# Channel-major x: first units on un-normed tokens, scaled per token afterwards

## The chip, the cores and the metric

The kernel runs on one core of a Trainium2 chip. The metric is the device time of one execution in microseconds (us), lower is better; three runs of the kernel before gave 838.16 to 839.91 us, median 838.94 us.

The core's engines are named as in the profile: PE (TensorE, matrix products into PSUM), ACT (ScalarE), DVE (VectorE), POOL (GpSimd), SP (SyncE, which here only issues transfers), and 16 DMA engines. Each engine works through its own list of instructions in the order of the program and waits where an operand is not there yet.

## What is computed

One decoder layer on 512 tokens of 1024 channels. All of it starts from one normed input `h`, and every projection is a slice of `h @ w_in`:

```python
def rmsnorm(x, g):
    y = x * lax.rsqrt(jnp.mean(x * x, axis=-1, keepdims=True) + EPS)
    return y * g
...
    h = rmsnorm(x, g_pre[i])
    (gq, gk, gv, ga, gz, dq, dk, dv, iq, ik, iw, dz, xq, xz, gates) = split_cols(h @ w_in[i])
    y_gla = gla_mixer(gq, gk, gv, ga, gz, ...)
    y_dsa = dsa_mixer(dq, dk, dv, iq, ik, iw, dz, rel_bias)
    y_mem = cross_mixer(xq, xz, rmsnorm(mem, g_mem[i]), w_mem_kv[i])
    ...
    x = x + rmsnorm(merged @ w_o[i], g_post[i])
```

The root mean square is a factor per token (a row of x) and `g_pre` a factor per channel (a column), so `(x * g_pre) @ w` multiplied per token by the factor `rstd` is `h @ w`.

## The kernel before, in words

**Arithmetic.** Every large product is taken in three: an operand is split into a high part (ACT copies it to the rounded type, helper `high`, line 95) and a low part (DVE subtracts the high part from the original, helper `low`, line 99 or, with a factor, 101), and high·high, high·low and low·high are added up in one PSUM bank (`mm3`, lines 108 to 110). `split` is `high` followed by `low`. So the list of each engine has the two halves of a split one after the other, and the `low` of DVE waits for the `high` of ACT.

**Units.** The projections are a list of units. A unit takes a weight block of 128 output channels (`unit_t`) or tokens by 256 channels (`unit_n`) and runs in four quarters; a chunk of weights is loaded (`load_next`), split (`split_next`, tiles `whi` and `wlo`) and used. In the loop at the end of `trunk` a unit's quarter is written, then the low halves of weights asked for before (`flush`), then the next weight split (`need`), then after the fourth quarter the unit's evaluation (`done`), then whatever `at(name, quarter, ...)` has put into this slot. Nothing reorders this afterwards: it is the order on every engine.

**The first units** are `dv` (values of the sparse branch), `pc` (a packed unit: indexer keys `ik`, the low-rank gate input `alow`, indexer weights `iw`), `gv0` (values of head 0 of the linear attention, `gv0.0` and `gv0.1`), then the indexer queries `iq0.0`, `iq0.1`, `iq1.0`, `iq1.1` and then `gqk0.0`. Between the quarters of `gv0.1` stand the four `gate_log(h)`: a product `pla` into one of three PSUM banks of the tag "at" (it needs `ar` and `uph`, which `gate_operands` makes), two ACT instructions (`ebig`) and one of DVE (`la_m`), which frees the bank. Unit outputs alternate between two PSUM banks of the tag "mm".

**The prologue** loads x token-major in eight pieces (tiles `x`, 128 tokens by 512 channels), and for each block of 128 tokens squares it on ACT (line 279), takes the power on POOL (273), scales on DVE (287), turns it over to channel-major by eight transposes on PE (294, `xps`) and splits it into `hh` and `hl`. `dv` starts when the first two blocks are turned.

**Transfers** before the loop all stand in SP's list; every one takes one of eight semaphores in turn and waits there for the transfer eight places earlier.

Of the kernel before, what the change touches and what calls it, by code (L numbers as in the profile page):

```python
# [57 lines left out]
def trunk(ctx, tc, x, mem, w_in, w_c, w_kv, w_out, w_o, cols, g_pre, g_mem, g_post, w_up, rel, onehot, out):  # L58
# [134 lines left out]
    def unit_n(name, first, lhs, tiles, done):  # L193

        o = []

        def quarter(q):
            if q == 0:
                o.append(psum("mm", name))
            n = len(tiles)  # L200
            if name[:2] == "dv":
                j, half = divmod(q, 2)
                co = o[0][:, 256 * j:256 * j + 256]
                wh, wl = chunks[first + half][3]
                for p in range(3):
                    for k in range(4):
                        ah, al = lhs(4 * half + k, tiles[j])
                        pe.matmul(co, al if p == 1 else ah, (wl if p == 2 else wh)[:, :, k],  # L208
                                  start=half + p + k == 0, stop=(half, p, k) == (1, 2, 3))
                return  # L210
# [89 lines left out]
    dvh, dvl = kv4("dvh", [4, 256], F32R), kv4("dvl", [4, 256], F32R)  # L300

    def dv_done(i, p):
        p3 = p.rearrange("p (t d) -> p t d", t=2)
        split(dvh[:, 2 * i:2 * i + 2], dvl[:, 2 * i:2 * i + 2], p3)

    win_n("dv", dv_done)
# [723 lines left out]
    xts = [[k2("yh", f"x{tt}{i}") for i in range(2)] for tt in range(4)]  # L1030
    xns = [[k2("acc", f"xn{tt}{i}") for i in range(2)] for tt in range(4)]

    def load_x(tt):
        for i in range(2):
            sp.dma_start(xts[tt][i], x[128 * tt:128 * tt + 128, 512 * i:512 * i + 512])

    with tc.manual_schedule():
        grow = w4("grow")
        sp.dma_start(grow[0:1], g_pre)
        load_x(0)  # L1040
        load_x(1)
        load_next(2)
        load_x(2)
        load_x(3)
# [11 lines left out]
        act.activation(warm[0:1], ones1[:, 0:1], AF.Square)
        gps = [psum("at", "gps") for _ in range(2)]
        for i in range(2):
            pe.matmul(gps[i], ones1, grow[0:1, 512 * i:512 * i + 512], start=True, stop=True)

        def h_scale(tt, ss):
            norm_scale(xts[tt], xns[tt], ss, gps)

        def h_turn(tt, tags=("tp", "tp")):
            t = slice(128 * tt, 128 * tt + 128)
            return norm_turn(xns[tt], lambda i: (hh[:, 4 * i:4 * i + 4, t],
                                                 hl[:, 4 * i:4 * i + 4, t]), tags)
# [18 lines left out]
        low2()
        low3 = h_turn(3, ("at", "ac"))
        low3()
        d0()
# [98 lines left out]
```

## Time and profile before

| | us |
|---|---|
| median of the runs (lowest, highest) | 838.94 (838.16, 839.91) |
| the profiled execution, its own time | 840.41 |
| its span, first to last instruction | 838.7 |
| PE busy in the span | 825.1 |
| first product of `dv` on PE | 12.9 |
| first product of `pc` | 28.2 |
| first product of `iq0.0` | 48.06 |
| first product of `iq1.0` | 56.41 |

The profiled execution ran 1.7 us longer than its span and 1.5 us longer than the median. Times in the rows below are from the start of the span. PE is busy nearly throughout; a wait of PE therefore lengthens the span, and work of the other engines matters where PE waits for it.

### The profile page before, as it was taken

How to read it: one execution, taken by the hardware profiler on the slowest of the kernel's cores; microseconds unless marked ns; L12 is line 12 of the kernel's file. 1: busy time of each engine (PE TensorE's matmuls, PEld its weight loads, DVE VectorE, ACT ScalarE, POOL GpSimd, SP SyncE). 2: the span in 40 equal slices, each digit the busy share in tenths (PEclk: the TensorE clock that was granted, in tenths of full speed). 3: DMA queues.
4: the chain of work that ended last, by engine and by line, in shares of the span. 5: the costliest groups of instructions: out<-in, count | busy, mean ns of one | idle time of the engine just before them, and what ended most of it. 6: DMA issues, size and time to landing. Idle time of an engine off the chain costs nothing.

```text
span 838.7 us, 10810 instructions
## 1 busy us (share of the span) xinstructions
PE 825.1 (98%) x4340; PEld 707.8 (84%) x4340; DVE 471.6 (56%) x839; ACT 329.1 (39%) x597; POOL 51.8 (6%) x77
## 2 busy tenths in 40 slices
PE   7999999999999999999999999999999999999997
PEld 5898888989888888888887888889989898888885
DVE  5578667777676545546677543445645554343623
ACT  5585555353433223334444422434334343322320
POOL 2000101000000020031122000000000000000000
PEclk9999999999999999999999999999999999999999
DMA  7333115221222222223122124232223241226402
GB/s 234 117 113 127 50 51 189 89 101 51 101 96 105 101 82 95 84 104 115 50 82 95 51 101 167 103 107 101 101 101 127 75 151 60 92 100 223 154 1 100
DMA packets 17101, 86.93 MB, mean 104 GB/s; under 512 B 2097, under 2 KB 2609, under 8 KB 8474
## 3 DMA queue, kind: packets, MB, share of 16 engines
q1 hardware_dynamic: 16474, 85.18, 29.1%
q10 hardware_dynamic: 576, 1.05, 0.3%
q8 instruction: 34, 0.56, 0.3%
q14 instruction: 17, 0.14, 0.1%
HBM read 83.03 MB, written 4.74 MB: 105 GB/s over the span
## 4 chain that ended last, share of the span: by engine, by line
PE 93%; DVE 2%; ACT 1%; issue 1%; DMA 1%; POOL 0%; SPq 0%; DVEq 0%; POOLq 0%; ACTq 0%
PE out L110 5%; PE out L108 5%; PE out L109 5%; PE pfin L110 2%; PE pfin L108 2%; PE pfin L109 2%; PE tpp L698 1%; PE dv.0_227 L208 1%; DMA x<-x 1%; PE dv.1_319 L208 1%; PE xps L294 1%; PE pov L109 1%; PE pa L560 1%; PE pov L110 1%; DVE wlo L99 1%
## 5 line engine op out<-in xcount | busy, mean ns | idle before, releaser
L99 DVE TENSOR_TENSOR wlo<-wraw,whi 128x1024 fp32r<-128x1024 f32 x133 | 166.0, 1249 | 78.2 <-ACT whi L95 77.4
L95 ACT ACTIVATE whi<-wraw 128x1024 fp32r<-128x1024 f32 x133 | 138.7, 1052 | 22.0 <-PE out L109 19.8
L108 PE MATMUL out<-yh,whi 128*128 128x512 f32 x192 | 75.3, 392 | 0.0
L110 PE MATMUL out<-yh,wlo 128*128 128x512 f32 x192 | 74.8, 390 | 0.0
L109 PE MATMUL out<-yl,whi 128*128 128x512 f32 x192 | 74.8, 389 | 0.0
L684 ACT ACTIVATE bm<-bm,nm 128x128 f32<-128x128 f32 (+3 forms) x32 | 18.0, 564 | 76.5 <-DVE nm L682 76.5
L668 POOL TENSOR_TENSOR bm<-toe,madd 128x128 f32<-128x128 f32 (+3 forms) x32 | 31.5, 1003 | 195.9 <-DMA toe<-bd 125.8
L110 PEld LDWEIGHTS out<-yh,wlo 128*128 128x128 f32 x192 | 36.0, 188 | 7.6
L108 PEld LDWEIGHTS out<-yh,whi 128*128 128x128 f32 x192 | 36.1, 188 | 7.3
L109 PEld LDWEIGHTS out<-yl,whi 128*128 128x128 f32 x192 | 36.1, 188 | 7.2
L273 POOL TENSOR_TENSOR rstd<-var,mhalf 128x1 f32<-128x1 f32 x10 | 5.5, 554 | 388.1 <-DVE var L929 289.7
L95 ACT ACTIVATE yh<-th 128x512 fp32r<-128x512 f32 x16 | 10.1, 632 | 46.5 <-DVE th L632 27.6
L492 DVE SCALAR_TENSOR_TENSOR gth<-gth,out 128x512 f32<-128x512 f32 x16 | 11.0, 687 | 28.1 <-PE out L110 28.1
L433 DVE MATCH_REPLACE8 madd<-m,madd 128x256 f32<-128x256 f32 (+2 forms) x48 | 25.6, 543 | 0.0
L429 DVE MAX8 m<-madd 128x8 f32<-128x256 f32 (+2 forms) x48 | 23.6, 547 | 0.0
L682 DVE CUSTOM_DVE_ANT_0 bm<-lg,bm 128x128 f32<-128x128 f32 (+3 forms) x32 | 15.5, 486 | 12.8 <-PE lg L110 12.5
L728 DVE TENSOR_TENSOR ydsa<-pov,th 128x128 f32<-128x128 f32 x32 | 7.8, 285 | 22.3 <-PE pov L110 22.3
L95 ACT ACTIVATE pth<-tpp 128x128 fp32r<-128x128 f32 (+3 forms) x32 | 13.7, 428 | 12.7 <-PE tpp L698 12.6
L99 DVE TENSOR_TENSOR yl<-th,yh 128x512 fp32r<-128x512 f32 x16 | 11.1, 693 | 11.2 <-ACT yh L95 11.2
L419 DVE SCALAR_TENSOR_TENSOR madd<-relu,iw,madd 128x256 f32<-128x256 f32 (+2 forms) x21 | 12.9, 616 | 7.6 <-ACT relu L415 7.1
L926 ACT ACTIVATE sq<-pfin 128x512 f32<-128x512 f32 x8 | 4.8, 598 | 31.2 <-PE pfin L110 31.2
L99 DVE TENSOR_TENSOR ptl<-tpp,pth 128x128 fp32r<-128x128 f32 (+3 forms) x32 | 15.4, 483 | 0.0
(1026 smaller groups left out, 2357.2 us busy)
## 6 DMA issues: line engine op xcount, KB each, us to landing
wraw<-w_in SPq DMA_DIRECT2D x43, 1024.0 KB, 4.7
wraw<-w_out SPq DMA_DIRECT2D x12, 1024.0 KB, 4.7
wraw<-w_kv SPq DMA_DIRECT2D x8, 1024.0 KB, 4.7
wraw<-w_o SPq DMA_DIRECT2D x4, 1024.0 KB, 4.8
bd<-bs SPq DMA_DIRECT2D x1, 2560.0 KB
x<-x SPq DMA_DIRECT2D x8, 256.0 KB, 6.3
toe<-bd SPq DMA_DIRECT2D x8, 256.0 KB, 4.9
xres<-x SPq DMA_DIRECT2D x4, 512.0 KB, 8.0
```

Of the source, the lines that this page charges most:

```text
L95: act.activation(hi, src, AF.Copy, scale=scale)
L99: dve.tensor_tensor(lo, src, f(hi), op=OP.subtract)
L108: pe.matmul(o, lh, rh, start=first, stop=False)
L109: pe.matmul(o, lh, rl, start=False, stop=False)
L110: pe.matmul(o, ll, rh, start=False, stop=last)
L208: pe.matmul(co, al if p == 1 else ah, (wl if p == 2 else wh)[:, :, k], start=half + p + k == 0, stop=(half, p, k) == (1, 2, 3))
L419: dve.scalar_tensor_tensor(sc, r[:, :n], iw[:, b, h:h + 1], sc, op0=OP.mult, op1=OP.add)
L429: dve.max(out=M8[b], in_=maskadd[b])
L433: dve.match_replace(out=maskadd[b], in_to_replace=M8[b], in_values=maskadd[b], imm_value=-FMAX)
L668: pool.tensor_tensor(bm[:, :n], Q[hp]["toe"][i][:, 384 - 128 * qb:512], maskadd[qb], op=OP.add)
L682: dve.tensor_tensor_reduce(out=bm[:, :n], in0=lg[:, :n], in1=bm[:, :n], scale=-1.0, scalar=FMAX, op0=OP.add, op1=OP.min, accum_out=nm)
L684: act.activation(bm[:, :n], bm[:, :n], AF.Exp, scale=-1.0, bias=nm, accum_out=su)
```

## The change

x is also handed over channel-major (`x_t`, made on the host by a transpose of the input's layout), in four tiles `xt` of 128 x 1024 (two channel blocks each). `g_pre` comes as eight columns of `cols`, loaded on ACT's queue. From `xt` the kernel makes `gh`, `gl`, the split of `x * g_pre` without the norm, and `dv`, `pc` and `gv0` take these; their outputs are multiplied by `rstd` per token, in the split for `dv` and `gv0` (token-major outputs, `rstd` as a column) and by one DVE product for `pc` (channel-major, so the factor is a row, spread over all partitions by four small products `rps` and one ACT copy `row`). The squares for `rstd` are taken from token-major x, loaded as four tiles. `h_norm(k)`, one for each of eight channel blocks, makes `hh`, `hl` from `xt` in the slots of `pc` and `gv0.0`: one DVE product with `g_pre` and `row`, one ACT copy, one DVE subtraction. The 32 transposes and the spreading of `g_pre` by PE go away; 12 products of zeros open PE's list. `dv` runs its 96 products in another order into four PSUM banks. The rows of the relative bias (`bias_rows`, four products `prel`) move from `gv0.0` to `iq1.0`, and their one-hot table is loaded in `iq0.0`.

```diff
+    def dv_done(tt, p):
+        split(R["dvh"][:, tt], R["dvl"][:, tt], p[:, :256], R["rstd"][:, tt:tt + 1])
...
+    def rstd_row():
+        p = psum("tp", "rps")
+        for tt in range(4):
+            pe.matmul(p[:, 128 * tt:128 * tt + 128], R["rstd"][:, tt:tt + 1].to_broadcast([128, 128]),
+                      ident, start=True, stop=True)
+        R["row"] = w2("row")
+        act.activation(R["row"], p, AF.Copy)
+
+    def h_norm(k):
+        xt = R["xt"][k // 2][:, k % 2]
+        dve.scalar_tensor_tensor(xt, xt, gpre[:, k:k + 1], R["row"], op0=OP.mult, op1=OP.mult)
+        split(hh[:, k], hl[:, k], xt)
...
-    def pc_done(p):
+    def pc_done(o):
+        p = w2("pc")
+        dve.tensor_tensor(p, o, R["row"], op=OP.mult)
...
-    at("pc", 3, lambda: None)
+    for k in range(8):
+        at(("pc", "gv0.0")[k // 4], k % 4, h_norm, k)
...
-    at("gv0.0", 1, bias_rows)
+    at("iq0.0", 0, bias_load)
+    at("iq1.0", 1, bias_rows)
...
+        for half in range(2):
+            sp.dma_start(wdv[:, half], loads[0][0][:, half])
+            for k in (2 * half, 2 * half + 1):
+                sp.dma_start(R["xt"][k], x_t[:, 2 * k:2 * k + 2])
+        sp.dma_start(xs[0], x[0:128])
+        sp.dma_start(xs[1], x[128:256])
         load_next()
+        sp.dma_start(xs[2], x[256:384])
+        sp.dma_start(xs[3], x[384:512])
...
+        for i in range(12):
+            pe.matmul(idle, zeros[:, 0:128], zeros, start=True, stop=True)
...
+        for half in range(2):
+            need(half, True)
+            for k in range(4 * half, 4 * half + 4):
...
+                split(gh[k], gl[k], R["xt"][k // 2][:, k % 2], gpre[:, k:k + 1])
+            dv_half(half, po)
+        ss, v = s8("ss", 4), s8("var", 4)
+        for tt in range(4):
+            act.activation(xs[tt], xs[tt], AF.Square, scale=1.0 / 32, accum_out=ss[:, tt:tt + 1])
+        dve.tensor_scalar(v, ss, EPS, None, op0=OP.add)
+        R["rstd"] = const.tile([128, 4], F32, name="rstd")
+        pool.tensor_tensor(R["rstd"], v, mhalf[:, :4], op=OP.pow)
+        rstd_row()
         need(2, True)
```

On DVE, before, the stretch from the keys of the indexer (`ikl`, behind `pc`) to the first two `la_m`:

```order
L99 TENSOR_TENSOR ikl<-pc,ikh 64x512
L99 TENSOR_TENSOR wlo<-wraw,whi 128x1024
L99 TENSOR_TENSOR ar<-alow,at__432 16x512
L99 TENSOR_TENSOR uph<-upraw,at__432 16x512
L99 TENSOR_TENSOR vl<-gv0.0_418,vh 128x512
L366 TENSOR_SCALAR la_m<-pla,col 128x512 x2
```

The end of the same stretch on DVE in the changed kernel, from `h_norm(4)`'s subtraction on (a line with `row` and the `hl` behind it are one `h_norm`):

```order
L99 TENSOR_TENSOR hl<-xt_113,hh 128x512
L99 TENSOR_TENSOR ar<-alow,at__408 16x512
L99 TENSOR_TENSOR uph<-upraw,at__408 16x512
L327 SCALAR_TENSOR_TENSOR xt_113<-xt_113,col,row 128x512
L99 TENSOR_TENSOR hl<-xt_113,hh 128x512
L327 SCALAR_TENSOR_TENSOR xt_114<-xt_114,col,row 128x512
L99 TENSOR_TENSOR hl<-xt_114,hh 128x512
L101 SCALAR_TENSOR_TENSOR vl<-gv0.0_391,rstd,vh 128x256 x2
L327 SCALAR_TENSOR_TENSOR xt_114<-xt_114,col,row 128x512
L99 TENSOR_TENSOR hl<-xt_114,hh 128x512
L393 TENSOR_SCALAR la_m<-pla,col 128x512 x2
```

Between `uph` and the first `la_m` stood one instruction and now stand eight; `h_norm(0)` to `h_norm(3)` stand ahead of this piece, the first three of them ahead of `ikl`.

On PE in the changed kernel, the end of `gv0.1` and the beginning of `iq0.0`, with the last of the four `pla`:

```order
L110 MATMUL gv0.1_472<-whi,gl_241 128x256
L108 MATMUL gv0.1_472<-whi,gh_244 128x256
L109 MATMUL gv0.1_472<-wlo,gh_244 128x256
L110 MATMUL gv0.1_472<-whi,gl_245 128x256
L389 MATMUL pla<-ar,uph 128x512 [waits DVE_49]
L108 MATMUL iq0.0_557<-hh,whi 128x384
```

The fourth `pla` stands directly ahead of `iq0.0` as it did before, and waits for a bank that the first `la_m` frees.

## Rows read from the trace of the kernel before

**Rows 1.** The page: the chain that ended last, by engine.

```profile
PE 93%; DVE 2%; ACT 1%; issue 1%; DMA 1%; POOL 0%; SPq 0%; DVEq 0%; POOLq 0%; ACTq 0%
```

**Rows 2.** Chain that ended last, 0 to 60 us: start, us, what.

```profile
28.39 0.23 PE pc L108
```

**Rows 3.** Timeline, PE: start, us, engine, line, operation, out<-in.

```profile
36.65 1.24 PE L449 MATMUL prel<-oh,relt 32*8 32x512 f32 x4
...
42.81 0.40 PE L362 MATMUL pla<-ar,uph 128*128 128x512 f32 x1
...
48.06 0.34 PE L108 MATMUL iq0.0_576<-hh,whi 128*128 128x384 f32 x1
...
56.41 0.33 PE L108 MATMUL iq1.0_659<-hh,whi 128*128 128x384 f32 x1
```

**Rows 4.** Stretches: busy by engine, then granted clock, DMA share, GB/s.

```profile
2.00:7.00 5.00, 3.75 (x4) 1.15 (x4) 0.68 (x2) 2.31 (x8) 2.63 (x8) 1.00 0.83 240
7.00:12.00 5.00, 2.65 (x11) 2.25 (x12) 2.54 (x6) 2.94 (x7) 0.56 (x1) 1.00 1.00 357
...
17.50:19.50 2.00, 2.00 (x19) 2.00 (x18) 1.34 (x4) 0.00 (x0) 0.55 (x1) 1.00 1.04 442
```

**Rows 5.** Timeline, SP and ACT: the first loads of x and their first reader.

```profile
1.20 1.79 SPq L1035 DMA_DIRECT2D x<-x  x4
...
4.22 0.63 ACT L279 ACTIVATE xn<-x 128x512 f32<-128x512 f32 x1 [1.94 <-DMA x<-x]
```

**Rows 6.** Timeline, ACT and POOL: from a square's sum to its power.

```profile
5.42 0.19 ACT L279 ACTIVATION_READ_ACCUMULATOR xn<-x 128x1 f32 x1
...
5.88 0.57 POOL L273 TENSOR_TENSOR rstd<-var,mhalf 128x1 f32<-128x1 f32 x1 [2.07 <-DVE var L284]
```

**Rows 7.** Instructions grouped by form: busy us, mean ns, idle before.

```profile
L99 DVE TENSOR_TENSOR wlo<-wraw,whi 128x1024 fp32r<-128x1024 f32 x9 | 10.9, 1216 | 1.1 <-ACT whi L95 1.1
L95 ACT ACTIVATE whi<-wraw 128x1024 fp32r<-128x1024 f32 x10 | 10.5, 1061 | 1.3 <-DMA wraw<-w_in 1.3
...
L591 DVE SCALAR_TENSOR_TENSOR S<-S,pd,kv 128x256 f32<-128x256 f32 x8 | 3.8, 475 | 0.0
```

**Rows 8.** Timeline near 121 us: a DVE product, its split on ACT and DVE.

```profile
120.96 0.75 DVE L632 SCALAR_TENSOR_TENSOR th<-to,col,th 128x512 f32<-128x512 f32 x1 [0.56 <-PE to L629]
121.74 0.63 ACT L95 ACTIVATE yh<-th 128x512 fp32r<-128x512 f32 x1 [2.07 <-DVE th L632]
...
122.41 0.69 DVE L99 TENSOR_TENSOR yl<-th,yh 128x512 fp32r<-128x512 f32 x1 [0.70 <-ACT yh L95]
```

**Rows 9.** Timeline behind `pc`, ACT and DVE.

```profile
33.95 0.59 ACT L95 ACTIVATE ar<-pc 16x512 fp32r<-16x512 f32 x1 [1.86 <-PE pc L110]
...
35.67 0.68 DVE L99 TENSOR_TENSOR ikl<-pc,ikh 64x512 fp32r<-64x512 f32 x1 [4.44 <-ACT ikh L95]
```

**Rows 10.** Timeline, ACT, first gate and `iq0.0`; DVE's first `la_m`.

```profile
43.24 0.69 ACT L364 ACTIVATE ebig<-pla,col 128x512 f32<-128x512 f32 x1 [1.08 <-PE pla L362]
43.97 0.75 DVE L366 TENSOR_SCALAR la_m<-pla,col 128x512 f32<-128x512 f32 x1 [1.07 <-ACT ebig L364]
...
53.58 0.49 ACT L95 ACTIVATE iqo<-iq0.0_576 64x384 fp32r<-64x384 f32 x1
54.10 0.55 DVE L99 TENSOR_TENSOR iql<-iq0.0_576,iqe 64x384 fp32r<-64x384 f32 x1 [2.02 <-ACT iqo L95]
```

**Rows 11.** Stretches of 4 us in the indexer's units, columns as in Rows 4.

```profile
56.00:60.00 4.00, 4.00 (x25) 4.00 (x24) 3.91 (x5) 2.13 (x4) 0.00 (x0) 1.00 0.39 69
...
68.00:72.00 4.00, 4.00 (x21) 3.37 (x20) 3.94 (x7) 2.35 (x4) 0.00 (x0) 1.00 0.79 291
```

**Rows 12.** Timeline, PE: products of `dv`, four in a row.

```profile
15.64 1.05 PE L208 MATMUL dv.0_227<-whi,hh 128*128 128x256 f32 x4
...
16.50 1.04 PE L208 MATMUL dv.0_227<-whi,hl 128*128 128x256 f32 x4
...
17.85 0.64 PE L208 MATMUL dv.0_227<-whi,hh 128*128 128x256 f32 x4
```

More of the change, by code (lines that the diff above doesn't have):

```diff
@@ L57, in trunk @@
 @with_exitstack
-def trunk(ctx, tc, x, mem, w_in, w_c, w_kv, w_out, w_o, cols, g_pre, g_mem, g_post, w_up, rel, onehot, out):
+def trunk(ctx, tc, x, x_t, mem, w_in, w_c, w_kv, w_out, w_o, cols, g_mem, g_post, w_up, rel, onehot, out):
     nc = tc.nc
@@ L200, in quarter @@
             n = len(tiles)
[L201 to L210, printed above, removed]
             for i in range(2 * n * q, 2 * n * q + 2 * n):
@@ L238, in win_n @@
         for i in range(2):
-            unit_n(f"{name}.{i}", first, h_lhs, (2 * i, 2 * i + 1), lambda p, i=i: done(i, p))
+            unit_n(f"{name}.{i}", first, lhs, (2 * i, 2 * i + 1), lambda p, i=i: done(i, p))
     ident = const.tile([128, 128], F32)
@@ L247, in trunk @@
     pool.memset(mhalf, -0.5)
-    ones1 = const.tile([1, 128], F32)
-    dve.memset(ones1, 1.0)
+    zeros = w2("zeros", F32R)
+    dve.memset(f(zeros), 0.0)
     rmask = k2("yl", "rmask")
@@ L297, in norm_turn, with dv_half @@
         return lambda: [low(dst(i)[1], pts[i], dst(i)[0]) for i in range(2)]
[L300 to L306, printed above, removed]
-    R = {}
-    def pc_done(p):
+    R = {}
+    def dv_done(tt, p):
+        split(R["dvh"][:, tt], R["dvl"][:, tt], p[:, :256], R["rstd"][:, tt:tt + 1])
+    win_n("dv", None)
+    def dv_half(half, po):
+        wh, wl = chunks[half][3]
+        for p, ks in ((0, (0, 1)), (0, (2, 3)), (1, (0, 1, 2, 3)), (2, (0, 1, 2, 3))):
+            for k in ks:
+                for tt in range(4):
+                    ah, al = g_lhs(4 * half + k, tt)
+                    pe.matmul(po[tt][:, :256], al if p == 1 else ah, (wl if p == 2 else wh)[:, :, k],
+                              start=half + p + k == 0, stop=(half, p, k) == (1, 2, 3))
+    def rstd_row():
[12 more added lines that the diff above has]
+        dve.tensor_tensor(p, o, R["row"], op=OP.mult)
         ikh, ikl = k2("yl", "ikh", F32R), k2("yl", "ikl", F32R)
@@ L351, in gv_done @@
         vh, vl = GV[h]
+        if h == 0:
+            for j in range(2):
+                tt = 2 * i + j
+                split(vh[:, tt], vl[:, tt], p[:, 256 * j:256 * j + 256], R["rstd"][:, tt:tt + 1])
+            return
         split(vh[:, 2 * i:2 * i + 2], vl[:, 2 * i:2 * i + 2], p.rearrange("p (t d) -> p t d", t=2))
-    win_n("gv0", lambda i, p: gv_done(0, i, p))
+    win_n("gv0", lambda i, p: gv_done(0, i, p), g_lhs)
     def gate_log(h):
@@ L443, in trunk, with bias_load @@
     bd = dr.tile([8, SKEW], F32, name="bd")
+    def bias_load():
+        R["oh"] = w4("oh", n=640)
+        sp.dma_start(R["oh"][0:32], onehot)
     def bias_rows():
@@ L1027, in trunk @@
         at(f"fin0{i}", 1, split_b, i)
[L1030 to L1035, printed above, removed]
-    with tc.manual_schedule():
[L1038 to L1044, printed above, removed]
+    with tc.manual_schedule():
+        R["xt"] = [w4(f"xt{k}").rearrange("p (k t) -> p k t", k=2) for k in range(4)]
+        xs = [kv4(f"x{tt}", [1024], F32) for tt in range(4)]
+        act.dma_start(col, cols)
+        wdv = wp.tile([128, 2, 1024], F32, name="wraw", tag="wraw", bufs=2)
+        loads[0][2] = wdv
+        state["load"] = 1
+        for half in range(2):
[4 more added lines that the diff above has]
+        sp.dma_start(xs[1], x[128:256])
         load_next()
-        sp.dma_start(col, cols)
+        sp.dma_start(xs[2], x[256:384])
+        sp.dma_start(xs[3], x[384:512])
         R["upraw"] = w2("upraw")
@@ L1051, in trunk @@
         sp.dma_start(R["relt"], rel)
-        R["oh"] = w4("oh", n=640)
-        sp.dma_start(R["oh"][0:32], onehot)
         warm = s8("warm", 1)
[L1056 to L1067, printed above, removed]
@@ L1086, in trunk @@
[L1086 to L1089, printed above, removed]
+        act.activation(warm[0:1], f(zeros)[0:1, 0:1], AF.Square)
+        idle = psum("ac", "idle")
+        for i in range(12):
+            pe.matmul(idle, zeros[:, 0:128], zeros, start=True, stop=True)
+        po = [psum(t, "dvps") for t in ("mm", "mm", "at", "at")]
+        for half in range(2):
+            need(half, True)
+            for k in range(4 * half, 4 * half + 4):
+                gh.append(k2("yh", f"gh{k}", F32R))
+                gl.append(k2("acc", f"gl{k}", F32R))
+                split(gh[k], gl[k], R["xt"][k // 2][:, k % 2], gpre[:, k:k + 1])
+            dv_half(half, po)
@@ L1090, in trunk @@
+        ss, v = s8("ss", 4), s8("var", 4)
+        for tt in range(4):
+            act.activation(xs[tt], xs[tt], AF.Square, scale=1.0 / 32, accum_out=ss[:, tt:tt + 1])
[3 more added lines that the diff above has]
+        rstd_row()
         need(2, True)
+        R["dvh"], R["dvl"] = kv4("dvh", [4, 256], F32R), kv4("dvl", [4, 256], F32R)
+        for tt in range(4):
+            dv_done(tt, po[tt])
```

45 lines of the change are left out of this document (15 added, 30 removed).

## The prediction, made before the changed kernel ran

> **What bounds the kernel now.** I read the page's chain first: 93% of what ended last is PE [rows 1], so the span moves by what PE waits for. The chain in order of time then shows where PE is late at the front: loads, norm and transposes stand ahead of `dv`, and `pc` begins at 28.4 in the chain (28.2 by the timeline) [rows 2]. From there PE issues without a gap: the gate products `pla` begin at 42.81, `iq0.0` at 48.06, `iq1.0` at 56.41, with 1.24 us of `prel` in between [rows 3]. So two questions decide: how much earlier `pc` begins, and whether ACT and DVE, which get new work between `pc` and `iq0.0`, still keep ahead of PE there.
>
> **The loads.** Before `rstd` is known, eleven loads of 0.524 MB must land (two of weights for `dv`, four of channel-major x, one for `pc`, four of token-major x): 5.77 MB, where before the first 1 MB of x was enough to begin. From 2.0 to 7.0 the DMA carried 240 GB/s, from 7.0 to 12.0 357 GB/s, and a load alone 442 GB/s [rows 4]. SP's first x load was its second transfer, at 1.20; now the first load stands first, at 0.79, so the flow begins about 0.4 us earlier. By 6.6 there are 1.20 MB, the other 4.57 MB at 357 GB/s take 12.8, so the last byte is in at 19.4. The first load landed 3.02 us after its issue [rows 5], while 0.262 MB at 240 GB/s from 2.0 on would be in at 3.1: its reader starts some 1.0 us behind the last byte. The last x tile is there at 20.4. Bounds: everything at 442 gives 15.8, everything at 240 gives 26.7.
>
> The Trainium skill's page "DMA: Bandwidth & Descriptors", section Specifications, gives 435 GB/s as the ceiling of the fabric; by that (an estimate) the last tile would land at 16.0 and the sum below would be 4.4 us less. The first 12 us of this trace stay well under it, only the load alone reaches it, so I don't use it for the sum.
>
> **From the last tile to DVE's first task.** Square of 1024 columns: like a weight's 1.06 [rows 7] plus 0.19 for its sum [rows 6], 1.25. From the end of the sum at 5.61 to the end of the power at 6.45 it took 0.84 [rows 6]. The four `rps`: `prel` has 640 columns in 1.24 [rows 3], 512 take 1.0. The copy `row`: 0.59 like `ar` [rows 9]. Then ACT splits `pc`'s weights, 1.06. Together 4.75: at 25.15 DVE can begin the low half of these weights. PE's own work is no term here: the 12 products of zeros (6144 columns, at 0.86 us for 1024 [rows 12] 5.2 us) are over before the first `gh`, which follows two loads (1.05 MB at 240 GB/s) and an ACT copy at about 7.6; without that cover they would cost their 5 us. The 96 products of `dv` are 0.47 us for four at the high clock and 0.86 at the low [rows 12], 11 to 21 us with the operands trickling in; they end between 19 and, if the clock rises in their midst, 24, against a power ready at 22.5, so `rps` may be up to 1.5 later.
>
> **`pc` and the gain.** `pc` needs one of the "mm" banks, which the first `dvl` frees: 25.15 + 1.22 + 0.45 = 26.8, some 1.4 us earlier than the 28.2 of before. That is all that PE gains here; `pc`, `gv0.0` and `gv0.1` keep their products, each as many columns as 48 of `dv`'s, 5.6 us.
>
> **DVE's list from 25.15.** The new piece is `h_norm`: product, ACT copy, subtraction, where DVE's subtraction waits for ACT, and the next product stands behind it. The trace has this very trio: 0.75, then 0.63 on ACT, then 0.69, with DVE idle for 0.70 in the middle [rows 8], 2.14 us from the first start to the last end; 0.05 overlaps the next, so 2.1 each, 16.8 for eight. In order, with 1.22 for a weight's low half and 0.475 (0.45 in a row) for 256 columns out of PSUM [rows 7]:
>
> a) `pc`'s weights 1.22, four `dvl` 1.8, the mask 0.2, first `gv0` weights 1.22: 29.6.
> b) `h_norm` 0 and 1, 4.2; second `gv0` weights 1.22; `h_norm` 2, 2.1; the product of `pc` with `row`, 0.7: 37.8. Before, `pc`'s evaluation began at 33.95 directly from PSUM [rows 9].
> c) ACT makes `ar`, `alow`, `ikh`, 1.72 from the first to `ikl` [rows 9], DVE waits, then 0.68: 40.2.
> d) `h_norm` 3, 2.1; a weight, 1.22; `h_norm` 4, 2.1: 45.6. Four small ACT copies of 0.63 follow its copy (44.9): 47.4; then `uph`, 0.68: 48.1. The first `pla` begins there, and stood at 42.81 before. PE, with `pc` from 26.8, `gv0.0` (and 2 of waiting for its second weights, done at 35.0), the `iwps` transposes, which wait for `alow` till 39.0, and two more quarters of 1.4, could be there at 42.2: it idles some 6 us.
> e) `h_norm` 5 and 6, 4.2; two `vl` 0.9; `h_norm` 7, 2.1; the first `la_m` 0.75: 56.1. The fourth `pla` waits for its bank, and `iq0.0` stands behind it: 56.4. Before it was 48.06 with `prel` ahead of it, whose 1.2 us now come later; with equal work done 46.9. PE is 9.5 us late.
> f) ACT's own list from `h_norm` 7 on (54.6): before, from the first `ebig` at 43.24 to the end of `iqo` at 54.07, it was 10.8 us without a gap [rows 10], now 0.3 more for `vh` in two pieces: 65.7. Two `iql` free the bank of `iq0.0` at 66.9, and `iq1.0` needs it: 67.0, against 55.2 (56.41 without `prel`). PE is 11.8 us late.
>
> Then DVE has no room to catch up: it is 3.91 to 3.94 of 4 us busy in each of the four stretches from 56 to 72 [rows 11], and after that PE, which had no waits to speak of, has nothing to give back. The later steps (bias rows moved, `onehot` loaded later) put the same 1.2 us of PE elsewhere and cost nothing: the rows are read by `bias_spread` in `gz1.0`, far behind.
>
> Sum: span 838.7 + 11.8 = 850.5; the profiled execution stood 1.5 above the median, so against that: 838.94 + 11.8 = **850.7 us**. Each microsecond in the landing of x moves it one for one; a trio between 1.8 and 2.3 moves it by -2.4 to +1.6.
>
> **Rivals.**
> *DVE is hidden and the earlier start stands.* If the eight `h_norm` disappear behind PE's 17 us of `pc` and `gv0`, only `pc`'s start counts: 1.4 us with the loads as in the sum, 6 with the fast bound; between them 3.7: 835.2. It decides at the first `pla`: `uph` would have to be done by 42, not 48. For it: DVE had room there, 4.44 us before `ikl` alone [rows 9]. Against it: 16.8 us of trios in list order, and idle time inside a trio can't be used. 8%.
> *Loads run at 442 from the start*, as the load alone did: 4.6 less, 846.1. For it: rows of 4 KB instead of 2 KB. Against it: nothing in the first 12 us did. 11%.
> *Loads stay at 240*: 6.3 more, 857.0. 6%.
> *PE's clock falls.* The clock column says 1.00 throughout [rows 4, 11], but the same four products are 0.86 us apart up to 16.5 and 0.47 later [rows 12], so PE began at the low of its two levels (1.2 and 2.4 GHz) and rose near 17.1, after working without a break since 11.3. Idling 6 us before the first `pla`, it could fall back; `iq0.0` and `iq0.1` take 8.35 us together [rows 3] and would last 0.86/0.47 as long, 6.9 us more, of which 2.2 are covered by the wait for `iq1.0`'s bank. Between nothing and 4.7, 2.3: 853.0. The Trainium skill says so on "TensorE: Matmul & The Clock Gate", section "HAM oscillation — how this bites in real kernels": a wait between bursts throttles PE again; no wait of that length behind the rise is in this trace. 8%.
>
> **How the numbers follow.** The forecast 64%, hidden 8%, fast loads 11%, slow loads 6%, clock 8%; the last 3% is for an end within 0.2% of before. The range goes from 844 (fast loads with cheap trios, 846.1 - 2.4) to 856 (short of the slow loads); outside lie the hidden case, the slow loads and some tails, 2 in 10. A measurement of this kernel can tell about 0.2% (1.7 us) from no change. Faster by more than that: only the hidden case, with most of its 8%, and a point for what I haven't seen: 0.08. Within: 0.04. Slower: 0.88.
>
> **What would show it.** Right: PE idle for several us directly before the first `pla` and again before the fourth, released by DVE `uph` and `la_m`; the trio's DVE idle near 0.7, released by ACT `hh`; `iq1.0` at about 67. Wrong: `pla` on time, or `rps` far from 22.5 to 24 (the loads), or products of `iq0.0` 0.32 apart (the clock).

## The result, and the profile after

The changed kernel takes 851.95 us (median of four executions, 851.83 to 852.09), the kernel before, on the same chip, 839.42 (838.16 to 839.91): 1.0152 times as long, 95% interval 1.0134 to 1.0169. That is 12.5 us slower. The profiled execution took 851.83 us with a span of 850.1, 11.4 more than the 838.7 of before; the two differences are 1.1 apart since the profiled execution of before (840.41) was longer than these.

The page of the changed kernel, the chain that ended last by engine (compare [rows 1]):

```profile
PE 87%; DVE 5%; ACT 3%; issue 3%; POOL 1%; DVEq 0%; POOLq 0%; ACTq 0%
```

PE's share fell from 93% to 87%; DVE, ACT and the issue of instructions took what it lost. Where PE waits, over the first 400 us (line, what it waited for, us, times, longest):

```profile
PE pla L389 <- DVE uph L99: 4.7, 1, 4.7
PE pc L108 <- DVE dvl L101: 3.3, 1, 3.3
...
PE iq1.0_642 L108 <- DVE iql L99: 1.7, 1, 1.7
PE rps L320 <- POOL rstd L1104: 1.6, 1, 1.6
...
PE pla L389 <- DVE la_m L393: 0.9, 1, 0.9
...
PE iq0.1_599 L108 <- DVE vl L101: 0.7, 1, 0.7
```

The rows shown all lie ahead of 67 us, and all but one are waits for DVE. The same on PE's timeline (compare [rows 3]); the last row is `prel` at its new place:

```profile
26.09 0.80 PE L108 MATMUL pc<-gh,whi 128*128 128x512 f32 x1 [3.29 <-DVE dvl L101]
...
46.81 0.79 PE L389 MATMUL pla<-ar,uph 128*128 128x512 f32 x1 [4.74 <-DVE uph L99]
...
55.16 0.50 PE L389 MATMUL pla<-ar,uph 128*128 128x512 f32 x1 [0.88 <-DVE la_m L393]
55.50 0.34 PE L108 MATMUL iq0.0_557<-hh,whi 128*128 128x384 f32 x1
...
66.72 0.41 PE L108 MATMUL iq1.0_642<-hh,whi 128*128 128x384 f32 x1 [1.72 <-DVE iql L99]
68.97 1.24 PE L481 MATMUL prel<-oh,relt 32*8 32x512 f32 x4
```

`pc` starts 2.1 us earlier than before, `pla` 4.0 later, `iq0.0` 7.4 later, `iq1.0` 10.3 later, and with `prel` still to come, 11.55 at equal work. DVE's timeline says why (one ACT row between; compare [rows 8, 9]):

```profile
28.40 0.74 DVE L327 SCALAR_TENSOR_TENSOR xt<-xt,col,row 128x512 f32<-128x512 f32 x1
29.18 0.63 ACT L95 ACTIVATE hh<-xt 128x512 fp32r<-128x512 f32 x1 [2.39 <-DVE xt L327]
29.84 0.69 DVE L99 TENSOR_TENSOR hl<-xt,hh 128x512 fp32r<-128x512 f32 x1 [0.70 <-ACT hh L95]
...
35.69 0.68 DVE L333 TENSOR_TENSOR pc<-pc,row 128x512 f32<-128x512 f32 x1
38.24 0.68 DVE L99 TENSOR_TENSOR ikl<-pc,ikh 64x512 fp32r<-64x512 f32 x1 [1.87 <-ACT ikh L95]
...
46.07 0.68 DVE L99 TENSOR_TENSOR uph<-upraw,at__408 16x512 fp32r<-16x512 f32 x1 [1.19 <-ACT at__408 L95]
...
56.52 0.75 DVE L393 TENSOR_SCALAR la_m<-pla,col 128x512 f32<-128x512 f32 x1 [1.41 <-ACT ebig L391]
```

The first three rows are an `h_norm`: product, ACT's copy, subtraction, with DVE idle for 0.70 before the subtraction. All eight look like this. `uph` ends at 46.8, and `pla` begins there.

Stretches (us, then PE, PEld, DVE, ACT and POOL busy, granted clock, DMA share, GB/s; compare [rows 4, 11]):

```profile
2.00:7.00 5.00, 4.99 (x12) 3.30 (x11) 0.63 (x1) 1.77 (x3) 2.09 (x7) 1.00 0.91 305
7.00:12.00 5.00, 4.17 (x31) 3.92 (x32) 4.67 (x7) 4.72 (x7) 0.00 (x0) 1.00 1.02 415
12.00:17.00 5.00, 5.00 (x44) 5.00 (x44) 2.54 (x4) 3.73 (x7) 0.00 (x0) 1.00 1.02 409
...
22.00:27.00 5.00, 1.72 (x10) 1.43 (x9) 2.58 (x5) 3.94 (x7) 0.00 (x0) 0.76 0.12 16
27.00:32.00 5.00, 5.00 (x14) 3.85 (x14) 3.60 (x7) 2.21 (x3) 0.00 (x0) 0.56 0.47 195
...
46.00:51.00 5.00, 4.19 (x17) 4.00 (x18) 3.50 (x6) 1.75 (x5) 0.00 (x0) 0.50 0.02 5
...
68.00:72.00 4.00, 4.00 (x21) 2.84 (x21) 3.87 (x6) 2.23 (x4) 0.00 (x0) 1.00 0.36 77
```

The loads ran faster than before; the granted clock fell to about half (0.50 is the lower of its two levels, 1.2 GHz) where PE had idled; and from 68 on DVE is full again.

### The profile page after: what moved, and what is told of

Same layout as the page of the kernel before. It is cut to its first block, busy times and chain, and to the rows that moved or that the text cites. A ratio compares the mean times of both kernels' runs of the same rounds, so it can differ in the third digit from the quotient of the medians.

```text
span 850.1 us, 10781 instructions
## 1 busy us (share of the span) xinstructions
PE 826.8 (97%) x4324; PEld 708.6 (83%) x4324; DVE 479.0 (56%) x849; ACT 335.6 (39%) x602; POOL 50.6 (6%) x74
## 3 DMA queue, kind: packets, MB, share of 16 engines
q10 hardware_dynamic: 720, 1.06, 0.3%
HBM read 85.12 MB, written 4.74 MB: 106 GB/s over the span
## 4 chain that ended last, share of the span: by engine, by line
PE 87%; DVE 5%; ACT 3%; issue 3%; POOL 1%; DVEq 0%; POOLq 0%; ACTq 0%
PE out L108 5%; PE out L110 5%; PE out L109 5%; PE pfin L110 1%; PE pfin L108 1%; PE pfin L109 1%; DVE wlo L99 1%; PE tpp L730 1%; DVE xt L327 1%; PE pov L109 1%; PE pa L592 1%; ACT hh L95 1%; ACT whi L95 1%; PE pov L110 1%; PE pov L108 1%
## 5 line engine op out<-in xcount | busy, mean ns | idle before, releaser
L273 POOL TENSOR_TENSOR rstd<-var,mhalf 128x1 f32<-128x1 f32 x6 | 3.3, 552 | 374.9 <-DVE var L961 289.7
L714 DVE CUSTOM_DVE_ANT_0 bm<-lg,bm 128x128 f32<-128x128 f32 (+3 forms) x32 | 15.5, 486 | 12.8 <-PE lg L110 12.5
## 6 DMA issues: line engine op xcount, KB each, us to landing
x<-x SPq DMA_DIRECT2D x4, 512.0 KB, 10.3
```

The lines of the kernel that those rows point to most:

```text
L714: dve.tensor_tensor_reduce(out=bm[:, :n], in0=lg[:, :n], in1=bm[:, :n], scale=-1.0, scalar=FMAX, op0=OP.add, op1=OP.min, accum_out=nm)
```

## The experiments

The theory: DVE's list in front of the second `iql` (low half of the queries of `iq0.1`), idle time in it included, sets the time, and behind that point nothing is won or lost. The rivals are in the expectations.

**1. The subtraction behind the next product.** DVE no longer stands still while ACT copies; the work is the same.

```diff
-        split(hh[:, k], hl[:, k], xt)
+        high(hh[:, k], xt)
+        if k:
+            low(hl[:, k - 1], R["xt"][(k - 1) // 2][:, (k - 1) % 2], hh[:, k - 1])
+        if k == 7:
+            low(hl[:, k], xt, hh[:, k])
```

> The changed kernel with one thing moved on DVE's list: in each h_norm the subtraction is put behind the next h_norm's product, so that DVE no longer stands idle while ACT copies. Nothing else differs. Theory (DVE's list sets when the gate products and iq0.0 can begin): eight idle times of 0.70 us go, less about 0.7 that the wait of uph for ACT gives back, 4.9 us: about 847.1 us (846.3 to 848.0), iq1.0 near 62. Rival A (the late landing of x and pc's start set the end): no change, 851.5 to 852.3. Rival B (the fallen clock of PE sets it): no change either.

Measured: 848.21 us (848.19 to 849.43), 1.0105 of before (1.0089 to 1.0122), 3.7 less than the change as it was. The direction is right, the size fell short by 1 us, and the time lies just outside the expected range. The idle times of 0.70 are gone from DVE's timeline. In the profiled execution two others have come, ahead of `pc`'s product and of `ar`, and the one ahead of `uph`, 1.19 in the change, has stayed:

```profile
34.89 0.69 DVE L337 TENSOR_TENSOR pc<-pc,row 128x512 f32<-128x512 f32 x1 [1.40 <-PE pc L110]
...
42.55 0.69 DVE L99 TENSOR_TENSOR ar<-alow,at__407 16x512 fp32r<-16x512 f32 x1 [0.75 <-ACT at__407 L95]
44.50 0.68 DVE L99 TENSOR_TENSOR uph<-upraw,at__407 16x512 fp32r<-16x512 f32 x1 [1.26 <-ACT at__407 L95]
```

DVE now arrives too early for PE's `pc` (which ran at the low clock) and for ACT's small copies.

**2. The same, with PE kept busy.** Seven and fifteen products of zeros around the `rps`, so that the clock doesn't fall before `pc`.

```diff
+        for i in range(7):
+            pe.matmul(idle, zeros[:, 0:128], zeros, start=True, stop=True)
         rstd_row()
+        for i in range(15):
+            pe.matmul(idle, zeros[:, 0:128], zeros, start=True, stop=True)
```

> The deferred subtraction once more, with 7 and 15 products of zeros ahead of and behind the four rps on PE, so that PE does not idle there. Theory: the deferred form fell some 2 us short of the sum since its DVE then waited 1.40 us for the last product of pc, which ran at the lower granted clock (1.2 GHz) after the idle time; with the clock kept at 1.00 from 22 to 27 this wait goes and the time is 1.2 to 1.4 below the deferred form: 846.9 (846.2 to 847.6), pla0 near 44.0 and iq1.0 near 62.9. Rival (another wait, of DVE for ACT, takes over at once): 847.9 to 848.5, iq1.0 still near 64.2.

Measured: 848.20 us (848.12 to 849.18), 1.0106 (1.0091 to 1.0121): no difference of the medians, so the expected 846.9 was missed and the time is the rival's, though `iq1.0`, at 63.00, is where the theory had it. The two profiled executions do differ as the theory says: the granted clock is 1.00 from 22 to 32, `pc`'s product no longer waits, `pla` begins at 44.04 instead of 45.23, and the span is 846.4 instead of 847.7. But the profiled execution of experiment 1 was the longest of its four; the other three had spans of 846.4 to 846.5 without products of zeros. No trace shows what PE did in those. Their mean granted clock is on record, 0.993 to 0.995 beside 0.990 in the longest, and in experiment 2 too the longest execution has the lowest (0.992 beside 0.995 and 0.996). That fits a cost of the clock in single executions, but doesn't show it: whether the clock cost 1.2 us in one of four, or something else did, stays open.

**3. The products on POOL.** Eight products of `xt` with `row` on POOL directly behind `row`; DVE keeps only the subtraction (with `g_pre`).

```diff
+        for k in range(8):
+            xt = R["xt"][k // 2][:, k % 2]
+            pool.tensor_tensor(xt, xt, R["row"], op=OP.mult)
...
-        dve.scalar_tensor_tensor(xt, xt, gpre[:, k:k + 1], R["row"], op0=OP.mult, op1=OP.mult)
-        split(hh[:, k], hl[:, k], xt)
+        split(hh[:, k], hl[:, k], xt, gpre[:, k:k + 1])
```

> The changed kernel with the eight products of h_norm taken by POOL, all directly behind row, by row alone; g_pre goes into the split as a factor. DVE's list loses eight products of 0.70 us and, since the high parts are there early, most of the idle time ahead of the subtractions. Theory (DVE's list): iq1.0 no longer waits, iq0.0 at about 47, the end 11 us earlier, about 840.5 us (839 to 843). Rival A (x lands late, pc starts late): pc is not earlier here, so no more than 1 us, 851 to 852. Rival B (clock): 850 to 852.

Measured: 846.21 us (846.17 to 846.24), 1.0082 (1.0067 to 1.0097): 5.7 less than the change, where 11.4 were expected. POOL's and DVE's timeline:

```profile
23.70 13.84 POOL L326 TENSOR_TENSOR xt<-xt,row 128x512 f32<-128x512 f32 x8 [1.92 <-ACT row L323]
...
25.97 1.65 DVE L101 SCALAR_TENSOR_TENSOR dvl<-dvps,rstd,dvh 128x256 fp32r<-128x256 f32 x4
...
28.44 2.31 DVE L99 TENSOR_TENSOR wlo<-wraw,whi 128x1024 fp32r<-128x1024 f32 x1
30.68 3.48 DVE L101 SCALAR_TENSOR_TENSOR hl<-xt,col,hh 128x512 fp32r<-128x512 f32 x2
34.09 2.31 DVE L99 TENSOR_TENSOR wlo<-wraw,whi 128x1024 fp32r<-128x1024 f32 x1
36.32 1.77 DVE L101 SCALAR_TENSOR_TENSOR hl<-xt,col,hh 128x512 fp32r<-128x512 f32 x1
```

While POOL worked (1.73 us a product), DVE's instructions with two operands in SBUF took about twice as long: a weight 2.31 instead of 1.22, an `hl` 1.74 instead of 0.75. `dvl`, which reads PSUM, kept its 1.65. From 38 on, with POOL done, a weight took 1.22 again. Two weights (2.2) and three `hl` (3.0) account for most of the shortfall. The Trainium skill says this on "SBUF — State Buffer", section "SBUF: two separate sides": a DVE instruction with two SBUF inputs and a GpSimd instruction that reads SBUF take turns on one pair of ports. This trace agrees, and POOL's products too took different times, 1.27 us for the shortest and 2.28 for the longest; my expectation had left it out.

**4. A second product behind the subtraction.** Eight more DVE products of 0.67 (start to start) in the same list, written to a tile that nobody reads.

```diff
         split(hh[:, k], hl[:, k], xt)
+        dve.scalar_tensor_tensor(R["spare"], xt, gpre[:, k:k + 1], R["row"], op0=OP.mult, op1=OP.mult)
```

> Every one of the eight h_norm gets a second copy of its DVE product, into a tile that nobody reads, directly behind the first. Theory (DVE's list sets the front): ACT's copy runs beside the second product, so the old idle 0.70 is filled and the subtraction comes about 0.05 to 0.1 later only; a trio then grows from 2.1 to at most 2.2 if the copy is released by the first product, and 8 x 0.05 to 0.1 = 0.4 to 0.8 us is all it costs; if the copy is released only behind the second product, a trio is 2.85 and the kernel is 8 x 0.75 = 6.0 later, 857 to 858.5. Both are the DVE list; which one it is shows in the idle time before hl (near 0 or near 0.7). Since the extra product writes another tile, the copy should not wait for it: 852.4 to 853.0 if it does not. Rival (the idle time inside the trio is not what costs, the products are hidden behind PE): no change, 851.7 to 852.2, with hl still waiting 0.7.

The kernel that ran has the second product behind the subtraction, not directly behind the first product as the expectation says; so what the expectation prices is experiment 5, and this one tests plain additional work. Measured: 855.97 us (855.92 to 856.03), 1.0196 (1.0179 to 1.0213), 4.0 more than the change. That is not 8 x 0.67 = 5.4, and DVE's timeline says where the rest is:

```profile
48.87 0.68 DVE L99 TENSOR_TENSOR uph<-upraw,at__414 16x512 fp32r<-16x512 f32 x1 [0.53 <-ACT at__414 L95]
...
60.63 0.75 DVE L395 TENSOR_SCALAR la_m<-pla,col 128x512 f32<-128x512 f32 x1 [0.74 <-ACT ebig L393]
```

`uph` waits 0.53 instead of 1.19 and the second `la_m` 0.74 instead of 1.41: 5.36 - 0.66 - 0.67 = 4.03. Work on DVE counts in full, less the idle time that it fills.

**5. The same second product in the gap.** Between the product and the subtraction, where DVE waited for ACT.

```diff
+        high(hh[:, k], xt)
+        dve.scalar_tensor_tensor(R["spare"], xt, gpre[:, k:k + 1], R["row"], op0=OP.mult, op1=OP.mult)
+        low(hl[:, k], xt, hh[:, k])
```

> The same second DVE product in every h_norm as in the doubled run (which had it behind the subtraction and cost 4.0 us), here between the product and the subtraction, so that it lies in the 0.70 us in which DVE waited for ACT's copy. Theory (what delays PE is DVE's list with its idle time, not the number of DVE's instructions): the product of 0.67 fills the gap, the subtraction starts at most 0.05 later, 8 x 0 to 0.05: 851.8 to 852.4, and DVE has no idle time left ahead of hl. Rival 1 (DVE's work counts wherever it stands): 4 us, as in the doubled run, 856. Rival 2 (ACT's copy and DVE's product slow each other down when they run side by side): ACT's copy over 0.63 and DVE's product over 0.74, hl later by as much.

Measured: 852.06 us (851.98 to 852.13), 1.0153 (1.0139 to 1.0166): the change's own time. In this kernel's timeline `hl` follows without a gap, and ACT's copy keeps its 0.63 beside DVE's product:

```profile
28.53 0.74 DVE L328 SCALAR_TENSOR_TENSOR xt<-xt,col,row 128x512 f32<-128x512 f32 x1
29.31 0.63 ACT L95 ACTIVATE hh<-xt 128x512 fp32r<-128x512 f32 x1 [2.38 <-DVE xt L328]
29.31 0.75 DVE L330 SCALAR_TENSOR_TENSOR spare<-xt,col,row 128x512 f32<-128x512 f32 x1
29.98 0.69 DVE L99 TENSOR_TENSOR hl<-xt,hh 128x512 fp32r<-128x512 f32 x1
```

The same eight instructions cost 4.0 us at one place and nothing at another: DVE's list with its idle time is what counts, not DVE's busy time.

**6. Less x to load.** The last two x tiles are not loaded, and the first two tiles are squared in their place, so this kernel leaves out the norm factors of tokens 256 to 511 (those of the first 256 tokens stand in).

```diff
-        sp.dma_start(xs[2], x[256:384])
-        sp.dma_start(xs[3], x[384:512])
```

> The changed kernel without the loads of the last two token-major x tiles; their squares are taken of the first two tiles instead, so the norm factors of tokens 256 to 511 are those of tokens 0 to 255 (this part of the computation is replaced). Four squares end near 18.3 instead of 20.3 us, and rps is then bound by the end of dv on PE at 19.9 instead of 21.65. Theory (everything from row on hangs on row, one for one): 1.7 us less, 850.2 us (849.8 to 850.7). Rival (what bounds the stretch to iq1.0 does not hang on row): 851.7 to 852.2.

Measured: 850.50 us (849.76 to 851.45), 1.0133 (1.0118 to 1.0149), 1.4 less than the change. In its profiled execution, the longest of four, the squares ended 1.9 us earlier (the last sum at 18.20 for 20.09), but the `rps` then stood behind `dv` on PE and began at 21.46; `row` came 0.30 earlier (22.55 for 22.85), `iq1.0` began 0.30 earlier (66.42 for 66.72), and the span was 0.4 shorter: one for one, but over 0.3 us only. `dv` itself was late there. PE had waited 1.63 for the first `gh`, 0.84 in the change, and the granted clock then fell:

```profile
7.00:12.00 5.00, 3.86 (x20) 3.70 (x21) 4.01 (x6) 4.41 (x7) 0.00 (x0) 0.72 1.02 411
```

In the change it is 1.00 in this stretch, and `dv` was over 1.62 us before the `rps` began. Two of the other executions took 849.76 and 849.89, 2.1 us less than the change, at a higher mean granted clock (0.993 and 0.994 beside 0.991 in the two longer ones). They have no trace, so it isn't shown that the whole 1.7 of the expectation came through in them.

**7. PE kept busy in all the gaps.** In addition to the products of zeros of experiment 2, 22 ahead of the first `pla`, on the change itself.

```diff
         p = psum("at", "pla")
+        if h == 0:
+            for i in range(22):
+                pe.matmul(R["idle"], zeros[:, 0:128], zeros, start=True, stop=True)
```

> The changed kernel with products of zeros in the three stretches in which PE idles: 7 ahead of rps, 15 behind it, 22 ahead of the first pla, so that PE's clock does not fall. Theory (PE has slack there, DVE's list bounds): pc ends some 2.7 us earlier, and the time stays: 851.7 to 852.4 us, iq1.0 at 66.7 as before. Rival B (the half clock in pc and gv0.1 is paid for): 2 to 4 us less, 848 to 850.

Measured: 852.15 us (851.91 to 852.98), 1.0154 (1.0139 to 1.0169). Stretches of this kernel:

```profile
22.00:27.00 5.00, 5.00 (x26) 4.09 (x27) 2.31 (x4) 3.89 (x7) 0.00 (x0) 1.00 0.11 15
27.00:32.00 5.00, 5.00 (x24) 4.14 (x23) 3.77 (x7) 2.15 (x4) 0.00 (x0) 1.00 0.53 197
...
46.00:51.00 5.00, 4.32 (x31) 3.78 (x30) 3.21 (x5) 2.04 (x5) 0.00 (x0) 1.00 0.00 2
...
55.00:59.00 4.00, 3.55 (x11) 3.45 (x12) 2.59 (x4) 3.94 (x7) 0.00 (x0) 0.50 0.00 0
```

The clock stays up where it fell to 0.76, 0.56 and 0.50, PE gets through its `pla` faster, and the fourth then waits 3.09 for `la_m` instead of 0.88, to begin at 55.45 instead of 55.16. Behind this longer wait the clock falls after all, one unit later: the products of `iq0.0` begin 0.32 apart (56.04, 56.36), and `iq1.0` begins at 67.00 without a wait for `iql`. So the low clock was moved, not removed; the time is the same with it in `pc` and `gv0.1` as with it in `iq0.0`, since PE was waiting for DVE anyway in the one case and just met `iql` in the other.

**8 to 10. Reordering the lists.** Each of these versions moves several things at once; the traces show which waits went, not what each move is worth. First the weights of `pc` ahead of the last two squares, so that `pc` starts directly behind `dv` (at 21.3), and the `h_norm`, in the form of experiment 1, spread up to `gv0.1`:

```diff
-        po = [psum(t, "dvps") for t in ("mm", "mm", "at", "at")]
+        po = [psum(t, "dvps") for t in ("mm", "at", "at", "at")]
...
+            if tt == 2:
+                need(2, True)
             act.activation(xs[tt], xs[tt], AF.Square, scale=1.0 / 32, accum_out=ss[:, tt:tt + 1])
...
+    at("pc", 0, rstd_row)
+    at("pc", 0, h_norm, 0)
+    at("pc", 0, need, 3)
+    at("pc", 1, h_norm, 1)
+    at("pc", 2, h_norm, 2)
...
+    at("gv0.1", 0, gate_log, 0)
+    at("gv0.1", 0, h_norm, 7)
```

> A version meant to beat both: the weights of pc are split ahead of the last two squares, dv uses one mm bank less so that pc starts directly behind dv near 20 us instead of behind the power and the row, the row is made in pc's first slot, the eight h_norm are spread from pc to gv0.1 with the subtraction behind the next product, and the low halves for the keys and the gate stand later. Theory (DVE's and ACT's lists set the front, and the change is slower because the h_norm stand ahead of what PE waits for): with DVE starting on this work some 4 us earlier and no idle time in the trios, iq0.0 begins at 43 to 46 and iq1.0 at 52 to 55 (55.2 before with equal work): 836 to 840. Rival (the sum of DVE's work in front of iq0.0 is the bound whatever its order): iq1.0 near 61, 846.

Measured: 843.90 us (843.63 to 844.23), 1.0052 (1.0037 to 1.0067). `iq0.0` begins at 46.35, level with before at equal work, but DVE and ACT come behind it: `iq0.1` waits 2.2 for `vl`, `iq1.0` begins at 59.03, and the time is 4 us over the expectation. DVE still waited 1.65 behind the first `h_norm`, 1.34 behind ACT's small copies, and 0.5 in each pair of `vl`. The next version fills these: `h_norm(1)` in `pc`'s first quarter, the copies of the constant operand before `pc` ends, both halves of `vh` copied ahead of the two subtractions.

> The version that starts pc early, mended where its trace still waited: the second h_norm stands in pc's first quarter (DVE idled 1.65 there), ACT makes the high halves of the gate's constant operand before pc ends (DVE waited 1.34 for a copy behind them), and the two halves of vh are both copied before the two subtractions (0.54 of waiting each time, two pairs). Theory (iql's time sets the end: 57.75 there, 54.10 before, and the time was 3.7 to 4.6 above before by nearly the same): the second la_m moves from 48.84 to about 44, iql to 53 to 54.5, iq1.0 begins near 54.5: 837.5 to 840, level with the kernel before. Rival (some other wait of ACT's list keeps the second ebig at 48): iql at 57, 843 to 844.

Measured: 840.98 us (840.78 to 841.39), 1.0024 (1.0015 to 1.0033), 1 us above the expected range. DVE still waits 2.02 ahead of the first `iql`, as in the kernel before [rows 10]: ACT has the logarithm of the gates (a table load of 1.28 and 1.06 of work) ahead of its copies of `iq0.0`. The last version puts it behind them, and the first two `gate_log` ahead of the last two `h_norm`:

```diff
-    at("gv0.0", 3, h_norm, 6)
-    at("gv0.1", 0, gate_log, 0)
-    at("gv0.1", 0, h_norm, 7)
-    for h in range(1, 4):
+    at("gv0.1", 0, gate_log, 0)
+    at("gv0.1", 0, h_norm, 6)
+    at("gv0.1", 0, gate_log, 1)
+    at("gv0.1", 0, h_norm, 7)
+    for h in range(2, 4):
...
-    at("iq0.0", 2, gate_ln, 0)
-    at("iq0.0", 3, gate_ln, 1)
+    at("iq0.0", 3, gate_ln, 0)
+    at("iq0.1", 0, gate_ln, 1)
```

> The mended version with ACT's list alone reordered further: the first two gate_log stand ahead of the last two h_norm (ACT idled 1.6 and 0.8 us there), and the logarithm of the gates (a table load of 1.28 and 1.06 of work) stands behind the copies of iq0.0 instead of ahead of them. Theory (what is left between this version, 1.9 us behind the kernel before, and the kernel before is ACT's list between the second ebig and iqo): iql moves from 54.5 to 51 to 52, iq1.0 from 55.8 to 52.5 to 54; DVE then waits for the logarithm until 53.4 where the first gate sum stood at 55.7, so 2.3 us at most come out: 838.7 (838.0 to 840.5). Rival (DVE's list from 55 on is the bound by itself, and it only waits elsewhere): 840.5 to 841.5.

Measured: 839.05 us (838.84 to 840.47) beside 839.57 (838.60 to 840.43), ratio 0.9999 (0.9990 to 1.0008): level with the kernel before. DVE's timeline in it:

```profile
51.90 0.55 DVE L99 TENSOR_TENSOR iql<-iq0.0_557,iqe 64x384 fp32r<-64x384 f32 x1
...
54.00 0.69 DVE L421 TENSOR_TENSOR la_m<-la_m,ebig 128x512 f32<-128x512 f32 x1 [0.97 <-ACT ebig L417]
...
57.16 0.55 DVE L99 TENSOR_TENSOR iql<-iq0.1_598,iqe 64x384 fp32r<-64x384 f32 x1
```

The wait of 2.02 became one of 0.97 for the logarithm. So order alone (with one PSUM bank of `dv` moved) brings back all of the 12.5 us, and no more in the versions tried. Its last step, the late logarithm, is open to the kernel before as well; that wasn't tried, so level here doesn't show that the change is free by itself: experiment 9, without that step, is 0.2% above the kernel before.

**All of them together.** The second `iql` on DVE, before, then changed, and the first product of `iq1.0` in experiment 10:

```profile
58.37 0.55 DVE L99 TENSOR_TENSOR iql<-iq0.1_616,iqe 64x384 fp32r<-64x384 f32 x1
...
69.70 0.55 DVE L99 TENSOR_TENSOR iql<-iq0.1_599,iqe 64x384 fp32r<-64x384 f32 x1
...
53.85 0.33 PE L108 MATMUL iq1.0_642<-hh,whi 128*128 128x384 f32 x1
```

Their starts in all kernels, the span of the profiled execution, and the span less each start:

| kernel | second `iql` | `iq1.0` on PE | span | less `iql` | less `iq1.0` |
|---|---|---|---|---|---|
| before | 58.37 | 56.41 | 838.7 | 780.3 | 782.3 |
| changed | 69.70 | 66.72 | 850.1 | 780.4 | 783.4 |
| 1 subtraction behind next product | 67.19 | 64.20 | 847.7 | 780.5 | 783.5 |
| 2 the same, PE busy | 65.99 | 63.00 | 846.4 | 780.4 | 783.4 |
| 3 products on POOL | 64.10 | 61.11 | 844.5 | 780.4 | 783.4 |
| 4 second product behind | 73.81 | 70.83 | 854.2 | 780.4 | 783.4 |
| 5 second product in the gap | 69.85 | 66.87 | 850.3 | 780.5 | 783.4 |
| 6 less x | 69.41 | 66.42 | 849.7 | 780.3 | 783.3 |
| 7 PE busy | 69.98 | 67.00 | 850.4 | 780.4 | 783.4 |
| 8 early `pc` | 62.02 | 59.03 | 842.5 | 780.5 | 783.5 |
| 9 waits filled | 58.81 | 55.83 | 839.2 | 780.4 | 783.4 |
| 10 late logarithm | 57.16 | 53.85 | 837.2 | 780.0 | 783.4 |

Over a spread of 16.7 us the difference to `iql` varies by 0.5, and all but 0.2 of that is experiment 10. The difference to PE's `iq1.0` varies by 0.2 in the changed kernels, experiment 10 included; before, it is 1.1 less, as `prel`'s 1.24 stood ahead of `iq1.0` there and not behind it. In experiment 10 `iq1.0` begins without a wait for `iql`, DVE reaches its second `iql` late because of the logarithm, and the span follows PE. So the theory is mended in one point: what counts is when PE begins `iq1.0`. In most versions that is set by `iql`, in experiment 10 by the wait of `iq0.1` for `vl` (1.96), in experiment 7 by PE's own low clock. Behind it nothing is given back or added: from 72.0 on PE idles for 8.0 us in the changed kernel, and from 61.7 on for 8.0 in the kernel before.

## Why the prediction was right, step by step

Forecast 850.7 (844 to 856), measured 851.95; forecast difference 11.8, measured 11.4 between the profiled spans and 12.5 between the medians.

| step | forecast | measured |
|---|---|---|
| last x tile's square begins | 20.4 | 19.12 |
| from there to DVE's first task | 4.75 | 5.30 |
| `pc` begins | 26.8 | 26.09 |
| a) first `h_norm` | 29.6 | 28.40 |
| c) `ikl` done | 40.2 | 38.9 |
| d) first `pla`, PE idle before it | 48.1, some 6 | 46.81, 4.74 |
| e) `iq0.0` | 56.4 | 55.50 |
| f) `iq1.0` | 67.0 | 66.72 |

**Right:** the mechanism and its places. `pla` waits for `uph`, its fourth for `la_m`, `iq1.0` for `iql`; from the first `ebig` (53.63) to the end of `iqo` (65.39) it is ACT's list that sets the pace, as step f) has it, with 0.74 of idle time in it; and the trio has the shape that the kernel before showed at 121 us [rows 8], with 0.70 of idle time in all eight. Experiments 4 and 5 show that it is the list with this idle time that counts, and the last table that the lost time was never given back. One sign came weaker than said: the fourth `pla` waited 0.88, not several us, because PE came to it late at the low clock; with the clock up it waited 3.09 (experiment 7).

**Mis-sized, in opposite directions:** x landed 1.3 us earlier, since the flow of the first 12 us was 305 and 415 GB/s, not the 240 and 357 that [rows 4] showed with smaller pieces; the truth lay between the sum's case and the rival of 442. The power on POOL took 1.04 for four columns, not the 0.57 of one [rows 6], most of the 0.55 by which the next step was longer than forecast. Step a) took 3.98, not 4.44, since each of DVE's instructions begins before the one ahead of it has ended (24.42 to 25.56 for the weights' 1.22). Between the first `pla` and `iq1.0` the forecast had 18.9 and the trace has 19.9: `vh` and `vl` in two pieces make DVE and ACT wait for each other, 0.54 on DVE and 0.7 on ACT in each pair, which I had priced at 0.3 of ACT alone. The sum ended 0.3 late of the trace because these nearly cancelled; that closeness is luck, the direction and the places are not. Small slips in the working don't bear on it: DVE is 3.87 to 3.94 of 4 us busy in the four stretches from 56 to 72, not 3.91 to 3.94, the two bounds for faster loads come to 15.7 and 15.9, not 15.8 and 16.0, and from the first of the four `rps` to `row` it took 1.2, not 1.0.

**The clock:** the rival that it falls in the gaps happened, already ahead of `pc` and again at `pla` (granted 0.56 from 27 to 32 and 0.50 from 46 to 51), and not where the rival put its price: the products of `iq0.0` stood 0.18 apart (55.50, 55.68, 55.86), not 0.32. The Trainium skill's page "TensorE: Matmul & The Clock Gate", section "HAM oscillation — how this bites in real kernels", which the prediction names, says that a wait between bursts throttles PE again; this trace agrees, behind waits of 3.29 and 4.74. In experiment 7 the products of `iq0.0` did stand 0.32 apart, and PE reached `iq1.0` 0.28 later than in the change. The rival's 2.3 us were not paid in either kernel: 852.15 and 851.95.

**The moves that were priced at nothing** (`prel`, the one-hot table) cost nothing that shows: `iq1.0` begins 11.55 later at equal work, and the span is 11.4 longer. The 12 opening products of zeros were over before the first `gh`, as said.

## What to carry to other kernels

An earlier start of the engine that bounds a kernel is worth only what the engines that feed it can follow: add up the new instructions in the feeder's list, with the idle time inside each split (product, copy, subtraction), up to the instruction where the bound engine first needs the result. If that list is longer than the cover, put independent work of the same engine into the idle time (here the next product, or other lists' copies earlier) before judging the idea. One instruction of the bound engine at the end of the disturbed stretch, followed through all variants, tells whether anything behind it matters; an instruction of a feeding engine does so only as long as the bound engine waits for it.

## What the runs showed of the hardware that I had not expected

DVE and POOL slow each other when both read SBUF: 1.22 became 2.31 and 0.75 became 1.74 on DVE beside POOL's products of 1.73 (1.27 to 2.28 each; experiment 3), while DVE's reads of PSUM kept their time (1.65 for four). ACT beside DVE showed nothing of the kind (0.63 in experiment 5). The granted clock fell to half around waits of PE of 3.29 and 4.74 us, and products of zeros in these waits kept it at 1.00 (experiment 7), where it fell to 0.50 behind the next wait, of 3.09, instead. And large first loads (rows of 4 KB) carried 415 GB/s from 7 to 12 us, where the kernel before, with rows of 2 KB for x, carried 357; that the rows are the reason wasn't tested.
